# A hybrid GLA and SSD layer on one core: two projections moved ahead in the fill queue, mask building moved between two loops

## The chip, the cores and the metric

The kernel runs on one core of one Trainium2 chip. Its time is device microseconds from start to end of one launch; the median of three runs of the kernel before is 1287.27 us. One further execution was profiled, and all durations below are from it. The engines are TensorE (PE; PEld is its weight load), VectorE (DVE), ScalarE (ACT), GpSimd (POOL) and SyncE (SP, which issues the DMAs).

## What is computed

One layer over 1024 latent tokens (d_model 1024) with a prefix of 256 context tokens. Normed and modulated tokens go through one input projection; its columns feed a gated linear attention (GLA, 4 heads) and an SSD (Mamba-2, 8 heads in 2 groups), both in both directions, and an output projection and a SwiGLU follow. Cut to the parts that matter here:

```python
def hybrid_mixer(h_ctx, h_lat, rows, w_in, ...):
    # q, k, v, r, lr, z, xbc, dt_raw = split(h @ w_in)
    fc = _stream_features(h_ctx, ...)
    fl = _stream_features(h_lat, ...)
    gla_c, gla_l = _bidir(_gla_scan, ...)   # q, k, v, gates g from lr
    ssd_c, ssd_l = _bidir(_ssd_scan, ...)   # conv + silu of xbc, step sizes dt
    ...
    return y_ctx, _merge_heads(fl, gla_l, ssd_l, ...)   # gated by r and z, normed, @ w_out
```

The step sizes are `dt = softplus(dt_raw + bias)`, the SSD decays are made from `a = dt * -exp(a_log)` and its running sums, and the GLA gates are `log_sigmoid(lr @ wg + bg) / 16`.

## The kernel before, in words

Products keep float32 accuracy by splitting each operand in a high and a low float16 part; one product is then three (`mm3`, lines 219 to 223). A projection of a 128-channel weight over 512 tokens is 24 such matmuls, and a unit of 128 tokens by 256 channels is 24 matmuls of half that length.

The work around the change runs in this order. (1) Conv inputs of the SSD (x4, x5, x0, x1) are projected. (2) From the projected step sizes (p48, line 694) DVE makes a chain of some 25 steps on 128x160 elements (lines 715 to 737) that ends in `av`. (3) `decays()` (line 557) transposes `lrt` on PE (L561) and multiplies `av` with triangular masks (L566 to L568); `decay_factors()` (line 579) goes on from there (L582, L598). (4) `level_masks()` (line 135) builds the 28 masks of the GLA's levels: two iotas, a copy of four triangles to float16 (L142), seven DVE steps (`bl`, L146) and 28 GpSimd products (`lvm`, L149). (5) The 3x3 convs run as taps: on DVE (L506), and for x5 as a ScalarE product (L518) and a GpSimd sum (L520). (6) For SSD group 0, `ssd_states` (line 843) makes 9 chunk states (first product L852), then `ssd_chunks` (line 863) goes over 8 chunks: scores (L875, L876), exp on ScalarE (L880), weights (L885, L887, L888), state products (L899) and the products with xsl, the finish (L913 to L919); after the fourth and the last chunk a norm (L925), after the sixth chunk and behind the loop a merge (`merge_T`, L627 to L630) of half the tokens each. (7) The same for group 1. (8) The GLA for each of two head pairs: gates (L1113 is the first product), levels, states, outputs.

Projections that aren't needed at once are put in a fill queue (`Feeder`, line 249). `F.fill(us)` takes units from its head until their nominal cost (2.6 us for a token unit, 5.2 for 512 tokens of a channel unit) exceeds the sum asked for; `F.need(name)` empties it up to that name. The numbers asked for stand in `FILLS` (line 41). Before, the queue holds z0 (8 units), k0 (5.2, 5.2, 2.6), q0 (5.2, 5.2), z1 (8), later r0 and r1 (8 each), then v0 (10 units). The first fill is 4.6 us behind the third conv input, then 2 us for each of group 0's states and 3.2 us for each of its chunks, 1.0 and 2.5 for group 1's.

A fill unit's result goes to one of two PSUM banks ("pf", `psum_f`, line 78); ScalarE copies it out (L311 for token units, L320 for channel units). z's units are copied into tiles of the tag "zg", which has two buffers of four units each:

```python
zg[g].append(ssd.tile([P, 4, 256], F32, tag="zg", bufs=2, name=f"zg{g}"))
...
qk_units(0)
z_unit(1)
st0 = ssd_states(0, FILLS[0])
F.need("z0")
```

z0 is held there, gated and normed in place, until its half is merged. The order on each engine is fixed when the program is built: a scheduler goes over the program in order and may let an instruction pass others when its buffers and inputs would be ready. On the chip each engine's instructions run in that order. The other tags that matter are "dk" (two buffers, SSD skip term; the masks' iotas use it), "xw" (three, weighted inputs; the masks' `bl` uses it), "wst" (three staged weights) and "whl" (four split weights).

Of the kernel before, what the change touches and what calls it, by code (L numbers as in the profile page):

```python
# [16 lines left out]
P = 128  # L17
D = 1024
KT = D // P
T = 1024  # L20
# [17 lines left out]
SL = 2048.0  # L38
SG = 16.0
EG = 1.0 / (16 * SG)  # L40
FILLS = (2, 1.0, 3.2, 2.5, 4.6, 3.4, 8, 8.0, 0.5, 4.6, 4, 5.0, 2.7, 3.4, 4.0)


@with_exitstack
def dit_layer_kernel(
# [89 lines left out]
    def level_masks():  # L135
        xi = ssd.tile([P, P], I32, tag="dk", bufs=2, name="xi2")
        xj = ssd.tile([P, P], I32, tag="dk", bufs=2, name="xj2")
        G.iota(xi, [[1, P]], base=0, channel_multiplier=0)
        G.iota(xj, [[0, P]], base=0, channel_multiplier=1)
        V.tensor_tensor(xi, xi, xj, ALU.bitwise_xor)  # L140
        for i, nm in enumerate(("le", "ge", "gt", "lt")):
            G.tensor_copy(t16[:, i], tri[nm])  # L142
        for li in range(7):
            lv = 64 >> li
            bl = ssd.tile([P, P], F16, tag="xw", bufs=3, name="bl")
            V.tensor_scalar(bl, xi, float(lv), None, ALU.is_lt)  # L146
            b4 = bl.rearrange("p (n a l) -> p n a l", a=2, l=lv)
            for i, (d, x, a) in enumerate(((0, 0, 1), (1, 0, 0), (0, 1, 0), (1, 1, 1))):
                G.tensor_tensor(lvm[:, li, d, x].rearrange("p (n l) -> p n l", l=lv),  # L149
                                t16[:, i].rearrange("p (n a l) -> p n a l", a=2, l=lv)[:, :, a], b4[:, :, a], MUL)  # L150
# [93 lines left out]
    def load_ch(c0, name):  # L244
        return load_w(w_in[:, c0:c0 + P], KT, P, name)
# [11 lines left out]
    class Feeder:  # L257
# [13 lines left out]
        def step(self):  # L271
            if self.cur is None:
                self._preload()
                if not self.ready:
                    return None
                self.cur = self.ready.pop()
                self._preload()
            cost = next(self.cur[1], None)
            if cost is None:
                self.done.add(self.cur[0])  # L280
                self.cur = None
                return 0.0
            return cost

        def fill(self, us):
            self.owed += us
# [240 lines left out]
    def conv_ctx(m, w):  # L527
        xc = ssd.tile([P, TC], F32, tag="xc", bufs=2, name=f"xc{m}")
        ps = proj_ch(w, *CTX, psum_f())
        S.activation(xc, ps[:, :256], AF.Copy, scale=INV)  # L530
        xcs[m] = xc
# [25 lines left out]
    def decays():  # L557
        for t0, t1 in ((0, 8), (8, 10)):
            ps = psum((P, 1024), F16)
            for t in range(t0, t1):  # L560
                PE.transpose(ps[:96, (t - t0) * P:(t - t0 + 1) * P], lrt[:, t, :], ident16)  # L561
            S.copy(LRT[:, t0 * P:t1 * P], ps[:96, :(t1 - t0) * P])
        pcs = psum()
        pc = pcs[:, :480].rearrange("p (a d n h) -> p a d n h", a=3, d=2, h=8)
        for d, (i_nm, e_nm) in enumerate((("le", "gt"), ("ge", "lt"))):
            PE.matmul(pcs[:, 80 * d:80 * d + 80], tri[i_nm], av80[:, d], start=True, stop=True)  # L566
            PE.matmul(pcs[:, 160 + 80 * d:240 + 80 * d], tri[e_nm], av80[:, d], start=True, stop=True)
            PE.matmul(pcs[:, 320 + 80 * d:400 + 80 * d], ones, av80[:, d], start=True, stop=True)  # L568
        S.activation(ecum, pc[:, 0], AF.Exp)
        S.activation(wdec, pc[:, 1], AF.Exp)  # L570
        for g in range(2):
            hg = slice(4 * g, 4 * g + 4)
            S.activation(etg[0:64, g], pc[0:64, 2, 0, 0:9, hg], AF.Exp)
            S.activation(etg[64:128, g, 0:2], pc[64:128, 2, 1, 1::-1, hg], AF.Exp)
            S.activation(etg[64:128, g, 2:9], pc[64:128, 2, 1, 9:2:-1, hg], AF.Exp)
        V.tensor_tensor(wdec, wdec, dt, MUL)

    def decay_factors():

        pcc = psum()[:, :128].rearrange("p (d n g h) -> p d n g h", d=2, n=NL, g=2)  # L580
        for d in range(2):
            PE.matmul(pcc[:, d], tric[d], e1[:, d, NC_CTX:], start=True, stop=True)  # L582
        X = ssd.tile([P, NL, 2, 2, 2, 4], F32, tag="Eh", bufs=2, name="X")
        rX = ssd.tile([P, 64, 4], F32, tag="Eh", bufs=2, name="rX")
        A = ssd.tile([P, 64, 4, 4], F16, tag="ti", bufs=2, name="A")
        for d in range(2):
            V.tensor_copy(X[:, :, :, d, 0], pcc[:, d])
            V.tensor_tensor(X[:, :, :, d, 1], lnd[:, d].rearrange("p n (g h) -> p n g h", g=2), X[:, :, :, d, 0], SUB)
        x64 = X.rearrange("p n g d y h -> p (n g d y) h")
        V.memset(A[:, :, 3], 0.0)  # L590
        S.copy(A[:, :, 0], x64)
        V.tensor_tensor(rX, x64, A[:, :, 0], SUB)
        S.activation(A[:, :, 1], rX, AF.Copy, scale=SL)
        V.scalar_tensor_tensor(A[:, :, 2], rX, SL, A[:, :, 1], MUL, SUB)
        a2 = A.rearrange("p (n q) s h -> p n (q s h)", n=NL)
        pT = psum((P, T), F16)
        for n in range(NL):
            PE.transpose(pT[:, n * P:(n + 1) * P], a2[:, n], ident16)  # L598
        S.activation(Lw, pT, AF.Identity, scale=isG, bias=cF)
        for h in range(4):  # L600
            S.activation(Rr[:, :, h], pT.rearrange("p (n i) -> p n i", i=P), AF.Identity, scale=hF[h], bias=hG[h])
# [89 lines left out]
    for t in list(range(2, 10)) + [0, 1]:  # L691
        for k in range(KT):
            src, o = (hc[k], t * P) if t < NC_CTX else (hl[k], (t - NC_CTX) * P)
            mm3(p48[:, t, :], src[:, 0, o:o + P], src[:, 1, o:o + P], w48[:, 0, k, :], w48[:, 1, k, :],
                k == 0, k == KT - 1)

    conv_ctx(4, wx[4])
    conv_ctx(0, wx[0])
    dt = feat.tile([P, 2, NCH, 8], F32, name="dt")
# [46 lines left out]
    V.tensor_scalar(e1, av, -250.0, None, ALU.max)  # L746

    wx[2] = load_ch(O_X + 2 * P, "x2")
    decays()
    decay_factors()  # L750
    level_masks()
    acc0, tp = taps(0)
    acc5, tp5 = taps(5, True)
    for a, b in zip(tp[:4], tp5[:4]):
# [48 lines left out]
    def z_silu(g):  # L803
        for z in zg[g]:
            tc.keep_in_program_order(S.activation(z, z, AF.Silu))

    qT, kT = [None, None], [None, None]

    def qk_units(p):
        def kd():  # L810
            if kT[p] is None:
                kT[p] = feat.tile([P, TT], F32, tag="kT", bufs=1, name=f"kT{p}")
            return kT[p]

        def qd():
            if qT[p] is None:
                qT[p] = feat.tile([P, T], F32, tag="qT", bufs=1, name=f"qT{p}")
            return _shift(qT[p])
        ch_unit(kd, O_K + p * P, (LAT0, LAT1, CTX), INV, f"k{p}")
        ch_unit(qd, O_Q + p * P, (LAT0, LAT1), INV * 0.125, f"q{p}")  # L820

    class _shift:


        def __init__(self, t):
            self.t = t

        def __getitem__(self, i):
            return self.t[i[0], i[1].start - TC:i[1].stop - TC]

    z_unit(0)
    new_xs(0)
# [118 lines left out]
        norm(1)  # L951
        return lambda: merge(1)

    qk_units(0)
    z_unit(1)
    st0 = ssd_states(0, FILLS[0])
    F.need("z0")
# [10 lines left out]

    tc.keep_in_program_order(S.preload_act_table_set(LN_EXP))
    last = ssd_chunks(0, st0, FILLS[2], side0)  # L970
    F.fill(FILLS[5])
    last()
    while sidew:
# [906 lines left out]
```

## Time and profile before

| | us |
|---|---|
| median of 3 runs (1281.62 to 1289.43) | 1287.27 |
| the profiled execution | 1286.45 |
| its span, first to last instruction | 1284.7 |
| PE busy | 1189.7 (93%) |
| DVE busy | 897.4 (70%) |
| ACT busy | 602.4 (47%) |
| POOL busy | 249.5 (19%) |

Busy time overlaps between engines, and matmuls overlap each other, so a row is an engine's own time, not a share of the whole. A stretch in which one engine is busy all the time is bound by it; where none is, the waits say which one is late. PEclk in the rows below is the granted clock of TensorE as a share of 2.4 GHz; 0.50 is 1.2 GHz.

### The profile page before, as it was taken

The numbers are of one execution on the slowest core, as the hardware profiler recorded it, in microseconds if no ns is written. First come the engines' busy times: TensorE is split into PE (matmuls) and PEld (weight loads), VectorE is DVE, ScalarE is ACT, GpSimd is POOL, SyncE is SP. The second block draws the span as 40 slices with busy tenths as digits, with TensorE's granted clock in tenths as the row PEclk, the third lists the DMA queues.
The fourth block names the chain that finished last, engine by engine and source line by source line (L and its number), as shares of the span: only waits on it lengthen the run. The fifth ranks groups of instructions, "written<-read, shape, count | busy, mean of one in ns | idle before, by whom it ended". The sixth has DMA issues, their size and how long they took to land. (4 is left out here: it accounts for less than half of the span.)

```text
span 1284.7 us, 21607 instructions
## 1 busy us (share of the span) xinstructions
PE 1189.7 (93%) x8684; PEld 673.5 (52%) x8684; DVE 897.4 (70%) x1486; ACT 602.4 (47%) x1158; POOL 249.5 (19%) x233
## 2 busy tenths in 40 slices
PE   5994899999999998999986899999999999999997
PEld 3553575767876697644442344444444444444444
DVE  8589796758378356776799865787775557754447
ACT  5345725545585464444673343444543334343433
POOL 0228032142000000001265211212211111300011
PEclk9997799999999999998988999999999999999999
DMA  9710211011201003488314522555532226320425
GB/s 307 215 29 17 70 30 50 18 34 46 95 6 35 1 3 100 149 285 303 117 50 148 179 91 74 164 184 176 181 115 67 66 81 212 133 91 17 148 75 203
DMA packets 90753, 140.20 MB, mean 109 GB/s; under 512 B 7592, under 2 KB 61597, under 8 KB 90653
## 3 DMA queue, kind: packets, MB, share of 16 engines
q1 hardware_dynamic: 90653, 138.82, 33.0%
q8 instruction: 68, 1.11, 0.4%
q14 instruction: 32, 0.26, 0.1%
HBM read 117.31 MB, written 20.97 MB: 108 GB/s over the span
## 5 line engine op out<-in xcount | busy, mean ns | idle before, releaser
L221 PE MATMUL ps<-T,wS 128*128 128x512 f16 x264 | 101.9, 386 | 10.5 <-DVE u L1612 7.0
L222 PE MATMUL ps<-T,wS 128*128 128x512 f16 x264 | 102.0, 386 | 4.0 <-DVE T L1441 4.0
L223 PE MATMUL ps<-T,wS 128*128 128x512 f16 x264 | 101.8, 386 | 0.0
L1722 DVE TENSOR_TENSOR ah<-hid,ah 128x512 f16<-128x512 f32 x66 | 50.6, 769 | 54.4 <-ACT ah L1721 54.4
L1501 DVE SCALAR_TENSOR_TENSOR wS<-S,wS 128x512 f16<-128x512 f32 x88 | 67.2, 777 | 27.9 <-ACT wS L1500 27.8
L1500 ACT ACTIVATE wS<-S 128x512 f16<-128x512 f32 x88 | 54.4, 628 | 56.9 <-PE ps L223 30.4
L1721 ACT CAST ah<-hid 128x512 f16<-128x512 f32 x66 | 40.5, 618 | 85.3 <-PE ps L223 46.5
L1501 DVE SCALAR_TENSOR_TENSOR wA<-wst,wA 128x512 f16<-128x512 f32 x66 | 55.9, 849 | 25.5 <-ACT wA L1500 25.4
L1500 ACT ACTIVATE wA<-wst 128x512 f16<-128x512 f32 x66 | 41.3, 628 | 54.4 <-PE ps L223 35.2
L222 PEld LDWEIGHTS <-wS 128*128 128x128 f16 x352 | 34.9, 99 | 55.1 <-issue 15.9
L221 PEld LDWEIGHTS <-wS 128*128 128x128 f16 x352 | 34.9, 99 | 50.7 <-DVE u L1612 7.6
L223 PEld LDWEIGHTS <-wS 128*128 128x128 f16 x352 | 34.9, 99 | 47.6 <-issue 7.5
L1517 POOL TENSOR_TENSOR S<-wst,S 128x512 f32<-128x512 f32 x22 | 32.6, 1483 | 137.2 <-DVE S L1516 91.5
L1515 POOL TENSOR_TENSOR S<-wst 128x512 f32<-128x512 f32 x22 | 31.0, 1409 | 117.3 <-DVE wS L1501 100.3
L506 DVE SCALAR_TENSOR_TENSOR acc<-xin,cwcol,acc 128x945 f32<-128x945 f32 (+2 forms) x40 | 48.9, 1240 | 0.4
L221 PEld LDWEIGHTS <-hl 128*128 128x128 f16 x448 | 42.5, 97 | 8.3 <-issue 3.1
L222 PEld LDWEIGHTS <-hl 128*128 128x128 f16 x448 | 42.5, 97 | 4.8 <-issue 0.8
L223 PEld LDWEIGHTS <-hl 128*128 128x128 f16 x448 | 42.5, 97 | 4.7 <-issue 0.4
L222 PEld LDWEIGHTS <-wA 128*128 128x128 f16 x264 | 25.9, 98 | 35.6 <-issue 5.2
L221 PE MATMUL ps<-wo,oT 128*128 128x512 f16 x112 | 44.2, 395 | 0.0
L222 PE MATMUL ps<-wo,oT 128*128 128x512 f16 x112 | 44.0, 393 | 0.0
L223 PE MATMUL ps<-wo,oT 128*128 128x512 f16 x112 | 43.8, 391 | 0.0
(540 smaller groups left out, 3539.0 us busy)
## 6 DMA issues: line engine op xcount, KB each, us to landing
wmst<-in_w_mod_dram SPq DMA_DIRECT2D x32, 512.0 KB, 4.8
wst<-in_w_gate_dram SPq DMA_DIRECT2D x26, 512.0 KB, 4.3
wst<-in_w_up_dram SPq DMA_DIRECT2D x26, 512.0 KB, 3.7
wdb<-in_w_down_dram SPq DMA_DIRECT2D x22, 512.0 KB, 5.6
x<-in_x_dram SPq DMA_DIRECT2D x16, 512.0 KB, 6.6
wm<-in_w_mod_dram SPq DMA_DIRECT2D x8, 1024.0 KB, 10.4
t32d<-wdt SPq DMA_DIRECT2D x11, 512.0 KB, 3.0
t14d<-wdt SPq DMA_DIRECT2D x11, 512.0 KB, 4.5
```

The costliest lines, as they stand in the source:

```text
L221: PE.matmul(ps, lh, rh, start=start, stop=False, skip_group_check=on)
L222: PE.matmul(ps, lh, rl, start=False, stop=False, skip_group_check=on)
L223: PE.matmul(ps, ll, rh, start=False, stop=stop, skip_group_check=on)
L506: V.scalar_tensor_tensor(acr[:, r0:r1, q0:q1], xr[:, r0 + dr:r1 + dr, q0 + dc:q1 + dc], cw, acr[:, r0:r1, q0:q1], MUL, ADD)
L1500: S.activation(w[:, 0], src, AF.Copy, scale=SW)
L1501: V.scalar_tensor_tensor(w[:, 1], src, SW, w[:, 0], MUL, SUB)
L1515: G.tensor_tensor(s3, b["A11"], b["A21"], SUB)
L1517: G.tensor_tensor(s4, b["A12"], s2, SUB)
L1721: S.copy(dst[:, 0], src)
L1722: V.tensor_tensor(dst[:, 1], src, dst[:, 0], SUB)
```

## The change

k0 and q0 lead the fill queue (their loads are begun at once, `step_ahead`), 13 us of fill are asked for ahead of `decays()` and 5 us behind it, the four triangle copies are taken out of `level_masks()`, and `level_masks()` is called behind group 0's loop, before its last merge.

```diff
-FILLS = (2, 1.0, 3.2, 2.5, 4.6, 3.4, 8, 8.0, 0.5, 4.6, 4, 5.0, 2.7, 3.4, 4.0)
+FILLS = (2, 1.0, 3.2, 2.5, 4.6, 3.4, 8, 8.0, 0.5, 4.6, 4, 5.0, 2.7, 3.4, 4.0, 5.0, 13.0)
...
         V.tensor_tensor(xi, xi, xj, ALU.bitwise_xor)
-        for i, nm in enumerate(("le", "ge", "gt", "lt")):
-            G.tensor_copy(t16[:, i], tri[nm])
         for li in range(7):
...
+        def step_ahead(self):
+
+            self._preload()
...
+    qT, kT = [None, None], [None, None]
+
+    def qk_units(p):
...
+    qk_units(0)
+    F.step_ahead()
     conv_ctx(4, wx[4])
     conv_ctx(0, wx[0])
...
     wx[2] = load_ch(O_X + 2 * P, "x2")
+    F.fill(FILLS[16])
     decays()
+    for i, nm in enumerate(("le", "ge", "gt", "lt")):
+        G.tensor_copy(t16[:, i], tri[nm])
+    F.fill(FILLS[15])
     decay_factors()
-    level_masks()
     acc0, tp = taps(0)
...
-    qk_units(0)
     z_unit(1)
     st0 = ssd_states(0, FILLS[0])
...
     last = ssd_chunks(0, st0, FILLS[2], side0)
+    level_masks()
     F.fill(FILLS[5])
     last()
```

`qk_units` and `_shift` are moved up in the text as they are. The lines of the kernel after differ by a few: L566 is L568 there, L627 is L629, L899 is L906, L1092 is L1099.

On PE around the decay products, the kernel before: `w_x_1300` is the weight of conv input x2, `av` the end of DVE's chain.

```order
L223 MATMUL pf<-hl_169,w_x_1300 128x512
L566 MATMUL ps<-av,trs 128x80
L567 MATMUL ps<-av,trs 128x80
L568 MATMUL ps<-av,ones 128x80
...
L582 MATMUL ps<-sp_1255,trs 128x64 x2
L221 LDWEIGHTS w_x_1300
L221 MATMUL pf<-hl_162,w_x_1300 128x512
```

The same place in the kernel after: `w_k_1193` and `w_q_1310` are the weights of k0 and q0, `w_x_796` that of x1, whose context part stood ahead of the decay products before.

```order
L221 MATMUL pf<-hc_171,w_k_1193 128x256
L563 LDWEIGHTS lrt
L563 MATMUL ps<-ident_81,lrt 96x128
...
L568 MATMUL ps<-av,trs 128x80
L569 MATMUL ps<-av,trs 128x80
L570 MATMUL ps<-av,ones 128x80
...
L219 LDWEIGHTS w_q_1310
L219 MATMUL pf<-hl_162,w_q_1310 128x512
...
L584 MATMUL ps<-sp_1260,trs 128x64 x2
L219 LDWEIGHTS w_x_796
L219 MATMUL pf<-hc_170,w_x_796 128x256
```

All of k0 (72 matmuls) now stands ahead of the decay products and the first half of q0 (24) behind them; the context part of x1 (24) and the first half of x2 (24) moved from ahead of them to behind.

On PE at the seventh and eighth chunk of group 0, the kernel after (`zg_1885` is the first half of z0, `w_z_0_1852` and `w_z_4_1857` are the two parts of z1's weight):

```order
L629 MATMUL ps<-ident,zg_1885 128x128 x4
L883 MATMUL ps<-cmc,bmc 128x128
L906 MATMUL ps<-st_1831,cmc 128x256
L906 MATMUL ps<-st_1831,cmd 128x256
L219 LDWEIGHTS hl_162
L219 MATMUL pf<-w_z_0_1852,hl_162 128x256
...
L221 LDWEIGHTS hl_169
L221 MATMUL pf<-w_z_4_1857,hl_169 128x256
L219 LDWEIGHTS Eh
L219 MATMUL ps<-xsl_1830,Eh 128x64
```

In the kernel before the same place has one unit of z1 between the first merge and the state products:

```order
L627 MATMUL ps<-ident,zg_1754 128x128 x8
L875 LDWEIGHTS Lw
L875 MATMUL ps<-Rr,Lw 128x512
...
L876 MATMUL ps<-cmc,bmc 128x128
L221 LDWEIGHTS hl_162
L221 MATMUL pf<-w_z_0_2250,hl_162 128x256
```

Between the state products (L906) and the products with xsl stand 96 matmuls of z1, four units, where the kernel before has none; between the scores of the third and of the eighth chunk, where it has one piece of k0, both of q0 and a unit of z1, there is no fill now.

On DVE at the end of group 1, the kernel before (`rv_y`, `ry_y` are the norm, `w_k_5183` and `w_q_5188` the weights of pair 1, `wg` the gate weights):

```order
L201 SCALAR_TENSOR_TENSOR ry_y_3638<-rt_y_3639,ry_y_3638 128x4
L630 SCALAR_TENSOR_TENSOR oT_3498<-ps,ncol,oT_3498 128x512
L630 SCALAR_TENSOR_TENSOR oT_3506<-ps,ncol,oT_3506 128x512
L216 SCALAR_TENSOR_TENSOR w_k_5183<-st_k_5181,w_k_5183 128x1024
L216 SCALAR_TENSOR_TENSOR w_q_5188<-st_q_5186,w_q_5188 128x1024
L1092 MEMSET wg_3785 96x512
L1097 TENSOR_SCALAR W_3793<-wg_3785 96x512
```

And the kernel after:

```order
L214 SCALAR_TENSOR_TENSOR w_k_5183<-st_k_5181,w_k_5183 128x1024
L920 TENSOR_TENSOR ti<-ps,ecum 128x256 x2
L214 SCALAR_TENSOR_TENSOR w_q_5188<-st_q_5186,w_q_5188 128x1024
...
L199 SCALAR_TENSOR_TENSOR ry_y_3750<-rt_y_3751,ry_y_3750 128x4
L1099 MEMSET wg_3785 96x512
L632 SCALAR_TENSOR_TENSOR oT_3610<-ps,ncol,oT_3610 128x512
L632 SCALAR_TENSOR_TENSOR oT_3618<-ps,ncol,oT_3618 128x512
L311 TENSOR_SCALAR v_3799<-pf 128x256
L1104 TENSOR_SCALAR W_3793<-wg_3785 96x512
```

The two splits moved into the last chunk, and the memset ahead of the merge's last steps.

## Rows read from the trace of the kernel before

**Rows 1.** Busy (instructions) by stretch: PE, PEld, DVE, ACT, POOL; PEclk, DMA share, GB/s.
```profile
92.00:112.00 20.00, 16.34 (x151) 11.82 (x147) 17.80 (x32) 12.18 (x17) 19.31 (x38) 0.91 0.10 27
112.00:127.40 15.40, 0.63 (x3) 0.12 (x2) 15.13 (x21) 6.43 (x7) 12.87 (x10) 0.64 0.00 0
127.40:146.00 18.60, 14.40 (x83) 10.07 (x84) 13.13 (x24) 16.71 (x30) 1.88 (x1) 0.78 0.00 1
146.00:174.00 28.00, 28.00 (x157) 18.66 (x155) 23.60 (x27) 12.42 (x21) 0.43 (x1) 0.80 0.43 113
...
203.30:246.60 43.30, 42.45 (x339) 25.32 (x339) 34.16 (x69) 24.41 (x49) 8.76 (x13) 1.00 0.08 25
...
264.00:323.70 59.70, 56.58 (x486) 39.00 (x487) 46.49 (x94) 28.25 (x62) 22.43 (x28) 1.00 0.14 39
323.70:348.50 24.80, 23.48 (x216) 20.76 (x213) 8.33 (x17) 13.75 (x25) 0.72 (x1) 1.00 0.22 64
```

**Rows 2.** Waits from 92 to 172 us; us in total, times, longest.
```profile
PE ps L566 <- DVE av L737: 14.8, 1, 14.8
...
PE pf L221 <- ACT w_x L215: 4.2, 1, 4.2
```

**Rows 3.** Busy time for tiles w_k (two rows), w_q, w_z, w_r; engines PE, PEld, DVE, ACT, or PE, DVE, ACT.
```profile
92.00:174.00 82.00, 0.00 (x0) 0.00 (x0) 1.23 (x1) 1.07 (x1) 0.79 0.17 45
174.00:264.00 90.00, 13.50 (x72) 6.81 (x72) 0.00 (x0) 0.00 (x0) 1.00 0.10 27
...
174.00:264.00 90.00, 10.71 (x48) 4.53 (x48) 0.00 (x0) 0.00 (x0) 1.00 0.10 27
...
92.00:174.00 82.00, 5.67 (x49) 2.44 (x2) 2.06 (x2) 0.79 0.17 45
...
323.70:349.00 25.30, 10.70 (x96) 0.00 (x0) 0.00 (x0) 1.00 0.22 66
```

**Rows 4.** Groups of 95 to 128 us (DVE), 92 to 174 (POOL); then DVE's timeline.
```profile
L146 DVE TENSOR_SCALAR bl<-xi 128x128 f16<-128x128 int32 x7 | 6.0, 851 | 0.5 <-POOL lvm L149 0.5
...
L149 POOL TENSOR_TENSOR lvm<-t,bl 128x64 f16<-128x64 f16 x28 | 12.5, 479 | 0.0
...
99.33 2.24 DVE L146 TENSOR_SCALAR bl<-xi 128x128 f16<-128x128 int32 x1
...
102.28 0.33 DVE L146 TENSOR_SCALAR bl<-xi 128x128 f16<-128x128 int32 x1
...
110.19 0.45 DVE L732 TENSOR_TENSOR sp<-sp,sp 128x160 f32<-128x160 f32 x1
...
125.60 0.32 DVE L732 TENSOR_TENSOR sp<-sp,sp 128x160 f32<-128x160 f32 x1
```

**Rows 5.** Timeline of PE, and of DVE for L888; start us, us, instruction.
```profile
100.00 0.27 PE L223 MATMUL pf<-hc,w_x 128*128 128x256 f16 x1
102.41 1.03 PE L561 MATMUL ps<-ident,lrt 128*96 128x128 f16 x10 [2.14 <-DVE lrt L724]
...
220.74 0.69 DVE L888 TENSOR_TENSOR Eh<-E,Eh 128x512 f16<-128x512 f32 x1 [0.68 <-ACT Eh L887]
...
229.13 0.68 DVE L888 TENSOR_TENSOR Eh<-E,Eh 128x512 f16<-128x512 f32 x1
...
251.72 0.49 PE L627 MATMUL ps<-ident,zg 128*128 128x128 f32 x3
```

**Rows 6.** Busy time by stretch behind the wait for `av`.
```profile
128.00:132.00 4.00, 4.00 (x18) 3.30 (x18) 0.91 (x6) 2.87 (x11) 0.00 (x0) 0.50 0.00 0
132.00:136.00 4.00, 4.00 (x16) 1.66 (x15) 2.50 (x4) 3.97 (x6) 1.88 (x1) 0.82 0.00 0
```

**Rows 7.** DVE's timeline at the end of group 1; in brackets the idle time before.
```profile
339.34 1.23 DVE L216 SCALAR_TENSOR_TENSOR w_k<-st_k,w_k 128x1024 f16<-128x1024 f32 x1 [5.12 <-ACT w_k L215]
...
347.24 0.42 DVE L1097 TENSOR_SCALAR W<-wg 96x512 f16<-96x512 f32 x1 [5.00 <-DMA wg<-in_gla_wg_b_dram]
...
350.60 1.29 DVE L1117 SCALAR_TENSOR_TENSOR gx<-ps,bt 128x512 f32<-128x512 f32 x2 [2.22 <-DMA bt<-in_gla_bg_b_dram]
```

More of the change, by code (lines that the diff above doesn't have):

```diff
@@ L695, in dit_layer_kernel, with kd, qd, __init__ @@
                 k == 0, k == KT - 1)
+    qT, kT = [None, None], [None, None]
+    def qk_units(p):
+        def kd():
+            if kT[p] is None:
+                kT[p] = feat.tile([P, TT], F32, tag="kT", bufs=1, name=f"kT{p}")
+            return kT[p]
+        def qd():
+            if qT[p] is None:
+                qT[p] = feat.tile([P, T], F32, tag="qT", bufs=1, name=f"qT{p}")
+            return _shift(qT[p])
+        ch_unit(kd, O_K + p * P, (LAT0, LAT1, CTX), INV, f"k{p}")
+        ch_unit(qd, O_Q + p * P, (LAT0, LAT1), INV * 0.125, f"q{p}")
+    class _shift:
+        def __init__(self, t):
+            self.t = t
+        def __getitem__(self, i):
+            return self.t[i[0], i[1].start - TC:i[1].stop - TC]
+    qk_units(0)
+    F.step_ahead()
     conv_ctx(4, wx[4])
@@ L805, in z_silu @@
             tc.keep_in_program_order(S.activation(z, z, AF.Silu))
[L807 to L829, printed above, removed]
     z_unit(0)
```

## The prediction

> **What bounds the kernel now.** I read the times by stage first, then the waits of the stretch that the change touches, then single engines inside it. By stage [rows 1], TensorE (PE) is nearly always busy from 146 us on and idle in one place: 0.63 us of work in the 15.4 us from 112 to 127.4, and 14.40 of 18.6 us behind it. The granted clock is 0.64, 0.78 and 0.80 in the stretches from 112 to 174 and 1.00 in those behind, so part of the work there runs at 1.2 GHz. The waits [rows 2] name the cause: 14.8 us in which the first decay product (L566) waits for `av`, the end of VectorE's (DVE's) chain of small steps, with all of PE's queue behind it; and 4.2 us for the split of the next conv weight. DVE is full there, 15.13 of 15.4 us [rows 1]. So 92 to 174 is bound by DVE and by PE's order; from 174 to 324 PE is the bound, as each gap of the SSD loops is filled with projections.
>
> **The change part by part.** It takes the projections of k and q of the first pair out of the loop of SSD group 0 and puts them before and behind the decay products: 13.50 and 10.71 us of PE [rows 3], 24.2 together. The masks leave the same stretch. The total work stays; only idle time and slow clock can be won. The sum goes along PE's order, by the profiled execution (1286.45 us: a span of 1284.7 and 1.75 around it; the median of the three runs is 0.8 above it).
>
> *First, the end of DVE's chain (127.4 us).* Seven mask steps, 6.0 us, go [rows 4]; the splits of k's and q's weights come in, 1.23 us each [rows 3]; net -3.5. Small DVE steps beside GpSimd's mask products are a little longer: L732 takes 0.45 us at 110 and 0.32 at 125.6 [rows 4]; some eight such steps are under the masks, so -1. I take `av` at 123.0, 4.4 us earlier. It can't help PE below 114.8, since k keeps PE until then (context products end at 100.3, k 13.5, the transposes L561 1.0 [rows 3, 5]); from the other side, GpSimd's eight conv steps stay, under which a DVE step is stretched (2.24 us against 0.33 for the same step [rows 4]), and they may bunch so that nothing is gained: 127.4.
> On this the Trainium skill (SBUF — State Buffer, Who interferes with whom) says that a DVE step with two SBUF inputs and a GpSimd step that reads SBUF take one shared port in turn, each for its whole length. [...] By the rule each of the 28 mask products (0.48 us) would also stop a DVE step beside it, for half its length on average, 0.24 us and not the measured 0.13; `av` would come some 1 us earlier still and the forecast would be 1 us lower. I go by the rows.
>
> *Second, from `av` to the first state product (174.0, where the fourth stretch of [rows 1] ends), 46.6 us before.* PE gets both halves of q there (10.7), and of what it did ahead of `av` before, the context conv of x1 (as k's context part, 13.50 - 10.71 = 2.8) and half of a projection like q's (5.4); two units of z0 go, 5.7 us [rows 3]: together +13.2. The wait of 4.2 us goes, since the conv weight is split far ahead in the new order. The slow clock goes in part: 0.78 over 18.6 us and 0.80 over 28 us [rows 1] are 8.2 and 11.2 us at the lower level; 15.2 of them are not the wait itself and cost half, 7.6 us. PE still idles some 8 us ahead of `av`, so the slow start repeats (0.50 and 0.82 in the two stretches behind the wait [rows 6]); I leave 2.7 of it: -4.9. Sum +4.1, so the first state product stands at 174.0 - 4.4 + 4.1 = 173.7. **Term: -0.3 us**, with k and q done.
> k's and q's loads go ahead of z's on SP's queue; the DMA share is 0.10 and 0.00 where they land [rows 1], so that costs nothing.
>
> *Third, the states of group 0* have 141 products of z in place of 143, and 48 before the first scores in place of k's 24 double-length ones. Nothing changes.
>
> *Fourth, the loop of group 0 and its end (203.3 to 264 us).* Here the fill is missing, and not replaced. z1's results go to the two zg buffers that z0 holds until each half is merged, so with two pf banks only two units can be done before the first merge. The order shows it: two units at the head of the loop, four between the seventh chunk's state products and its last products, two behind the second merge. With nothing between, a chunk goes at the pace of DVE and the waits between engines. DVE has 34.16 us in the loop [rows 1], by my count 5.0 of them for splits, merge and norm: 3.7 per chunk. From the fourth to the sixth L888, the one place where two chunks' products stand on PE without fill between, there are 8.4 us [rows 5], 4.2 per chunk. I take 4.2; the bounds are 3.7 and the 5.4 of now (43.3 / 8). The first products come 7.2 us after the first scores, the seventh's at 7.2 + 5.5 x 4.2 = 30.3; four units of 24 products, 2.8 us each, and the last two outputs: 42.5. From there to the second merge 5.1 us as now (246.6 to 251.72 [rows 5]), and 0.9 for the masks' first steps, which stand among the norm's on DVE: 48.5. It came at 48.4. Behind it PE has two units of z and four of r, 144 products of 0.111 us (r's 96 take 10.70 [rows 3]), 16.0, and 4.4 for merge, transposes and the first xw: group 1 starts at 68.9 against 60.7. **Term: +8.2 us.** In return 98 products of r are done, against 8.
> The masks, 12.5 us on GpSimd [rows 4], are done at about 62, ahead of group 1's xw, so they cost nothing; without that cover xw would wait for what is left of them.
>
> *Fifth, group 1* (59.7 us [rows 1]): the same fills, 8 products more: **+0.9 us**.
>
> *Sixth, from the last outputs of group 1 to the first gate product L1113 (323.7 to 348.5, 24.8 us [rows 1]).* Before, 96 products of r and 109 of v stand here; now 80 of v, 8.9 us, with the merge 10.0. What is late next is the gate weight. Its memset on DVE stood behind the splits of k1 and q1, which waited 5.12 us for ScalarE [rows 7]; in the new order these are done in the loop and the memset follows the norm: 4.4 us for the norm, 0.5, 5.0 for the loads (the wait of L1097 [rows 7]), 1.2 for W, with the issues 12.0. **Term: 12.0 - 24.8 = -12.8 us.**
>
> *Seventh, the gates.* The bias load goes ahead of the weights on SP's queue, so of the wait of 2.22 us at L1117 [rows 7] 1.5 go; 29 products of v (3.2 us) are left over and run among the levels, where some gaps take 1.0 of them: **+0.7 us**. Behind this everything is as before and shifts.
>
> Sum: -0.3 + 8.2 + 0.9 - 12.8 + 0.7 = -3.3, that is 1283 us. Of the 30 us that were idle (22.6 by [rows 1]) or slow (7.6) ahead of 174, most come back as idle time in the loop, where PE has some 2 us of work in a chunk of 4.2.
>
> **The rivals.**
> A. *The fill moves over whole*: the loop runs at DVE's 3.7 us, and the last outputs don't wait for the four z units. For it: DVE is busy for only 79% of the loop. Against it: PE's order is fixed and has these units ahead of the outputs. It takes off up to 11.2 us: 1272.
> B. *The z1 units jam PE, and it is slower than before*: units three to six need pf banks that ScalarE empties only when the first half is merged. If that merge comes 1.5 chunks later than I think, the four units, and both last outputs behind them in PE's queue, come 1.5 x 4.2 = 6.3 us later: +3.0, 1289.5. It decides if the second merge comes later than 52 us behind the first scores. For it: ScalarE's order has the two evacuations behind the norm's four scalings; against it: they stand ahead of the merge's own copies.
> C. *DVE's chain is not shorter*, as GpSimd's conv steps stretch other steps instead: `av` at 127.4, +4.4: 1287.5, no change.
>
> **How the numbers follow.** Forecast 0.45 (its own range 1278 to 1289), A 0.18, B 0.17, C 0.20. By the bounds of the chunk's pace alone (5.5 chunks of 3.7 to 5.4 us) the time is 1280 to 1290. The range, 1271 to 1294, leaves out the far half of A and the tail of B. A measurement of this kernel tells about 1% (12.9 us) from no change: faster 0.14 (most of A), slower 0.04 (B with group 1 late as well), within 1% 0.82.
>
> **What would show it.** Right: PE's wait ahead of the decay products falls from 14.8 to about 8 us and `av` ends near 123; the first state product stays within 2 us of 174; PE's busy share in group 0's loop falls from 98% to some 75%; group 1 starts 7 to 9 us later than before; L1113 comes 3 to 4 us earlier. Wrong: group 1 starts no later than before (A), the second merge comes over 52 us behind the first scores (B), or `av` ends at 127 (C).

## The result and the profile after

The changed kernel takes 1296.08 us in the median (1294.41 to 1297.61); beside it the kernel before takes 1287.48. The ratio is 1.0069 with a 95% interval of 1.0054 to 1.0084: slower, by 0.7%. The forecast was 1283 us, a little faster, with 1294 as the end of its range. The profiled execution took 1294.93 us, with a span of 1293.2 against 1284.7.

One point serves as a yardstick below: the first product of `kht` (gated keys times v, where the states of the GLA begin; L1188 before, L1195 after). Up to there PE has done the same work in either kernel: z, r, v, k and q of the first pair and both SSD groups. By stage, the kernel before (columns as in [rows 1]; the stretches are group 0 from its first scores to group 1's first state product, group 1's last outputs, that is the last products with xsl, to the first `kht` product, and the whole way from 92 us):

```profile
203.30:264.10 60.80, 59.61 (x494) 40.69 (x493) 40.92 (x82) 34.74 (x74) 9.94 (x15) 1.00 0.08 23
323.75:386.80 63.05, 58.53 (x957) 51.13 (x954) 35.40 (x54) 43.77 (x84) 0.72 (x1) 1.00 0.16 52
92.00:386.80 294.80, 262.32 (x2527) 189.76 (x2522) 216.74 (x362) 162.82 (x304) 83.70 (x106) 0.94 0.14 40
```

The kernel after, with the stretch up to the first state product ahead:

```profile
92.00:173.50 81.50, 68.83 (x445) 43.09 (x446) 66.19 (x90) 50.38 (x75) 23.16 (x19) 0.94 0.19 52
203.00:274.80 71.80, 64.83 (x488) 47.27 (x487) 41.05 (x90) 32.80 (x73) 19.64 (x45) 0.81 0.11 30
334.60:393.50 58.90, 51.73 (x863) 43.80 (x860) 37.21 (x59) 41.78 (x81) 0.72 (x1) 0.91 0.16 46
92.00:393.50 301.50, 270.70 (x2507) 193.94 (x2507) 213.78 (x361) 161.50 (x301) 79.04 (x106) 0.92 0.14 39
```

The whole way grew from 294.8 to 301.5 us, by 6.7. PE's idle time in it did not grow (294.8 - 262.3 = 32.5 before, 30.8 after); PE was busy for 8.4 us more with nearly the same products (the cut at 92 us falls at another one). The extra busy time is half clock: the granted clock over the way fell from 0.94 to 0.92, and it moved. Whether that is also the cause of the loss is tested below. Ahead of the first state product it rose (0.79 over 82 us [rows 3], 0.94 after); in group 0's stretch it fell from 1.00 to 0.81, and behind group 1 from 1.00 to 0.91. The first of these two stretches is 11.0 us longer than before. The other is only 4.2 us shorter, although 96 products of r, 10.7 us, have left it.

The start went as forecast. Of PE's waits from 92 to 172 us, the two that answer to [rows 2]:

```profile
PE ps L568 <- DVE av L765: 9.7, 1, 9.7
PE pf L219 <- ACT xc L532: 1.7, 1, 1.7
```

The wait for `av` fell from 14.8 to 9.7 us, the wait of 4.2 us for the conv weight is gone. Group 0's loop from its first scores on, in short stretches:

```profile
203.00:210.00 7.00, 7.00 (x59) 5.38 (x58) 4.73 (x7) 6.09 (x8) 0.00 (x0) 1.00 0.26 77
210.00:216.00 6.00, 4.90 (x46) 2.82 (x46) 6.00 (x14) 2.38 (x6) 2.18 (x3) 1.00 0.28 87
216.00:222.00 6.00, 5.57 (x35) 3.00 (x34) 6.00 (x14) 2.29 (x5) 2.43 (x3) 0.56 0.00 0
222.00:228.00 6.00, 6.00 (x28) 3.23 (x26) 6.00 (x15) 3.26 (x9) 2.87 (x4) 0.50 0.00 0
228.00:234.50 6.50, 6.30 (x31) 3.10 (x30) 4.51 (x14) 4.65 (x12) 1.46 (x2) 0.50 0.01 3
234.50:240.00 5.50, 5.50 (x40) 4.45 (x40) 3.49 (x7) 2.26 (x6) 1.39 (x2) 0.76 0.00 0
240.00:248.00 8.00, 7.86 (x87) 6.69 (x85) 1.20 (x4) 0.38 (x1) 0.00 (x0) 1.00 0.01 2
248.00:253.00 5.00, 0.10 (x1) 0.11 (x1) 3.63 (x14) 2.19 (x8) 2.26 (x7) 0.78 0.00 0
253.00:258.00 5.00, 5.00 (x24) 3.70 (x25) 2.58 (x6) 3.11 (x8) 5.00 (x20) 0.54 0.00 0
```

This table is the heart of the case. Up to 210 us PE still has two units of z1. From 210 to 228 DVE is busy without a gap (18.0 of 18.0 us) and PE has nothing but the chunks' own small products; the granted clock goes to 0.56 and then 0.50, so PE looks busy (11.57 of 12 us from 216 to 228) with work that would fill half of that. From 234.5 to 248 it is the other way round: PE works through four units of z1 and DVE is busy for 4.7 of 13.5 us. From 248 to 253 PE waits for the second merge's norm, and from 253 on it is mostly PE again, with the work that the queue could not run earlier. That z1 waits for room is seen on ScalarE, which copies the first two units out of their banks at 233 us, behind the first merge's transposes (L629), though PE ended them at 206.5 and 210.0:

```profile
233.07 0.66 ACT L313 ACTIVATE zg<-pf 128x256 f32<-128x256 f32 x2 [1.47 <-PE ps L629]
```

Before, both kinds of work stood side by side (42.45 of 43.30 us of PE beside 34.16 of DVE [rows 1]); now they stand one after the other.

PE's timeline at three points (start, duration, then the wait in brackets), the second merge of group 0, the first gate product and the first `kht` product:

```profile
252.90 2.15 PE L629 MATMUL ps<-ident,zg 128*128 128x128 f32 x8 [5.04 <-ACT zg L932]
...
353.97 1.04 PE L1120 MATMUL ps<-W,LRT 96*128 96x256 f16 x8
...
393.46 0.77 PE L1195 MATMUL ps<-v,kht 128*64 128x128 f32 x10
```

And DVE's timeline at the end of group 1, where [rows 7] had the memset behind the splits:

```profile
334.64 0.42 DVE L925 TENSOR_TENSOR zg<-zg,ti 128x256 f32<-128x256 f32 x1
334.98 1.22 DVE L214 SCALAR_TENSOR_TENSOR w_k<-st_k,w_k 128x1024 f16<-128x1024 f32 x1
...
336.93 1.55 DVE L214 SCALAR_TENSOR_TENSOR w_q<-st_q,w_q 128x1024 f16<-128x1024 f32 x1
...
342.43 0.16 DVE L199 SCALAR_TENSOR_TENSOR ry_y<-rt_y,ry_y 128x4 f32<-128x4 f32 x1
345.80 0.48 DVE L1099 MEMSET wg<- 96x512 f32 x1 [3.22 <-PE ps L629]
...
351.65 0.42 DVE L1104 TENSOR_SCALAR W<-wg 96x512 f16<-96x512 f32 x1 [3.79 <-DMA wg<-in_gla_wg_b_dram]
```

The splits of k1 and q1 (L214) stand inside the last chunk, ahead of the norm's last step (L199, 342.43), and the memset of the gate weight waits 3.22 us for L629, the transposes of the merge. From the gate product to `kht` PE has next to no gap any more:

```profile
353.97:393.46 39.49, 38.20 (x774) 33.16 (x771) 27.74 (x39) 30.16 (x60) 0.00 (x0) 1.00 0.02 5
```

### The profile page after: what moved, and what is told of

It reads as the page before. It is cut to its first block, busy times and chain, and to the rows that moved or that the text cites. A ratio compares the mean times of both kernels' runs of the same rounds, so it can differ in the third digit from the quotient of the medians.

```text
span 1293.2 us, 21601 instructions
## 1 busy us (share of the span) xinstructions
PE 1198.6 (93%) x8684; PEld 676.4 (52%) x8684; DVE 896.7 (69%) x1487; ACT 601.3 (46%) x1157; POOL 246.3 (19%) x233
## 5 line engine op out<-in xcount | busy, mean ns | idle before, releaser
L220 PE MATMUL ps<-wo,oT 128*128 128x512 f16 x112 | 45.1, 402 | 0.0
L219 PE MATMUL ps<-wo,oT 128*128 128x512 f16 x112 | 45.0, 402 | 0.0
L221 PE MATMUL ps<-wo,oT 128*128 128x512 f16 x112 | 44.7, 399 | 0.0
```

The lines of the kernel that those rows point to most:

```text
L219: PE.matmul(ps, lh, rh, start=start, stop=False, skip_group_check=on)
L220: PE.matmul(ps, lh, rl, start=False, stop=False, skip_group_check=on)
L221: PE.matmul(ps, ll, rh, start=False, stop=stop, skip_group_check=on)
```

## The experiments

They ran in three series, each on one chip and each beside the kernel before, whose median was 1290.1, 1290.9 and 1290.9 us there; ratios are to it. The kernel before, profiled once more, was up to 1.5 us earlier ahead of the first state product (`av` ended at 126.0 against 127.4), kept the times of the trace shown within 0.8 us from there to 640 us, and was 3.5 us later at the end of the MLP's weight steps (last L1501 at 1057.3 against 1053.8). So times from the first state product to 640 us are compared directly, `av` to no better than 1.5 us, and whole times by ratio.

**The two kernels again.**

> The kernel before, unchanged, for a profile beside the others. All theories: up to 640 us within 1 us of the trace shown (first gate product near 348.5); if the chip is the cause of the 5 us that the four profiles so far lose between 640 and 1055, this one loses them too.

> The changed kernel, unchanged, for a profile on the chip of these runs. All theories: first kh product (L1195) within 1 us of 393.5, loop at +71 to +72.5, span 1296 to 1298, as the kernel before was 3.4 us longer here.

Measured: the kernel before, span 1288.1, first gate product 348.6, first `kht` product 386.3; the changed kernel, span 1296.9, `kht` 394.1, group 0's stretch 71.6 us. Both as expected; the loss is 7.8 us at `kht` and 8.8 at the end, so nearly all of it arises up to there.

**The masks alone.** The kernel before with

```diff
-        for i, nm in enumerate(("le", "ge", "gt", "lt")):
-            G.tensor_copy(t16[:, i], tri[nm])
...
     decays()
+    for i, nm in enumerate(("le", "ge", "gt", "lt")):
+        G.tensor_copy(t16[:, i], tri[nm])
     decay_factors()
-    level_masks()
...
     last = ssd_chunks(0, st0, FILLS[2], side0)
+    level_masks()
```

> The kernel before with only the masks (and the four casts) moved behind group 0's loop; k and q stay in the loop. Theory (the loss is the fill taken out of the loop, the masks are harmless): av ends 3 to 4 us earlier, near 124; the first state product some 3 us earlier than 174.0; group 0's loop and the end of group 1 keep their lengths (60.7 and 24.8 us); time 1283 to 1285. Rival (the masks' steps behind the loop cost: DVE's mask steps among the norm, GpSimd's products ahead of group 1's products): the stretch from the first scores to group 1's first state product is 3 us or more longer than 60.7, and the time is 1287 or more.

Measured: ratio 0.9989 (0.9977 to 1.0001). `av` ended at 121.2, the first state product came at 168.3, 5.7 us earlier; group 0's stretch took 61.4 us, the one from group 1's last outputs to the first gate product 25.1.

```profile
92.00:168.30 76.30, 58.20 (x370) 40.09 (x370) 64.97 (x88) 47.34 (x71) 22.17 (x18) 0.82 0.19 49
197.60:259.00 61.40, 60.01 (x494) 40.76 (x493) 42.79 (x90) 34.80 (x74) 18.01 (x45) 1.00 0.08 23
92.00:381.60 289.60, 261.55 (x2505) 189.19 (x2505) 213.96 (x359) 162.43 (x302) 79.36 (x105) 0.95 0.14 41
```

The rival falls: behind the loop the masks cost 0.6 us. What they win ahead of it is more than expected, 5.7 us, and 5.2 of it are there at the first `kht` product (381.6 for 386.8). At the end the ratio leaves 1.4 us (0.0011 of 1290), with an interval from nothing to 3.0, so the 2 to 4 us that were forecast are not confirmed. Beside the second profile of the kernel before, the lead is 4.7 us at `kht`, 5.0 at 550 us, 2.7 at 570 and 1.9 from 930 on: most of what is lost goes between the second head pair's last merge and the MLP's first weight step. What takes it there is not shown.

**The lead alone.** The changed kernel with `level_masks()` back behind `decay_factors()`.

> The changed kernel with the masks back in their old place, k and q still leading. Theory (the masks' move wins 4 us at av and costs nothing): av near 127.5, PE's wait ahead of the decay products some 14 us in place of 9.7, the first state product near 177, loop and end as in the changed kernel; time 1298 to 1301. Rival (the masks behind the loop cost what is lost): group 1 starts under 9 us later than in the kernel before, and the time is 1293 or less.

Measured: ratio 1.0104 (1.0084 to 1.0123), 1303.1 us. `av` 127.9, first state product 178.2, `kht` 397.0, group 0's stretch 70.8. As the theory had it, with a first state product 1 us later still; only PE's wait ahead of the decay products was not the 14 us expected but 9.2, with another 3.2 inside k's projection. So the loss belongs to the lead of k and q, and the masks take some 4 us off it (ratios 1.0104 and 1.0069).

**The gate weight early.** The changed kernel with a staging buffer for weight and bias, loaded ahead of group 1's loop:

```diff
+    stg = wp.tile([P, 1024], F32, tag="wst", bufs=3, name="stg")
+    wg32 = stg[:96, 0:512].rearrange("p (d n) -> p d n", d=2)
+    V.memset(wg32, 0.0)
...
     F.need("z1")
     z_silu(1)
...
+    G.tensor_copy(bt, bts)
```

> The changed kernel with the gate weight and the bias loaded into a staging buffer ahead of group 1's loop, so that only the split of W and a copy of the bias stand behind the merge. Theory (W's chain of memset behind the merge, loads of 5 us and split sets the first gate product): it comes at 346 to 349 in place of 354.0, and the time is 1288 to 1291. Rival (the products of v at the lower clock, behind the wait for a pf bank, set it): the first gate product stays at 352 or later, time 1294 to 1297.

Measured: ratio 1.0084 (1.0059 to 1.0110). The first gate product (L1123 here) came at 350.8, 3.2 us earlier than in the changed kernel, and the first `kht` product (L1198) at 395.6, no earlier (393.5 and 394.1 in the two profiles of the changed kernel). This run stood 1 us later already at group 0's first scores; counted from group 1's last outputs the gate product came at 15.2 us for 19.3, and `kht` at 59.9 for 58.8. PE's timeline:

```profile
350.84 1.04 PE L1123 MATMUL ps<-W,LRT 96*128 96x256 f16 x8
...
355.69 0.27 PE L219 MATMUL pf<-w_v,hl 128*128 128x256 f16 x1 [2.93 <-ACT v L313]
...
395.58 1.09 PE L1198 MATMUL ps<-v,kht 128*64 128x128 f32 x16
```

Both numbers of the theory fail, and the rival's as well. W's chain was a real wait, but behind the gates PE now stands 2.93 us for ScalarE, which empties v's bank among the gates' own steps, and 2.3 us more for the gates, where the changed kernel has no such wait; and all of v must still be done ahead of `kht`. The gate product was the wrong place to count a gain at.

**Fill put back into the loop.** r's second half goes out to DRAM by a small buffer and needs no room that the loop holds:

```diff
+    r1_unit()
     z_unit(1)
     st0 = ssd_states(0, FILLS[0])
...
     r_unit(0)
-    r1_unit()
```

> The changed kernel with r's second half (whose results go out to DRAM by a small buffer) put ahead of z1 in the fill queue, so that group 0's loop has a unit of fill in each chunk again. Theory (the loop without fill is the loss): PE is busy for 95% or more of the loop at a granted clock of 1.00, group 1's first state product comes at 263 to 266 in place of 274.8, the end of group 1 takes some 19 us as in the changed kernel; time 1284 to 1287. Rival (the work is only shifted, the idle time turns up in another place before the gates): the first gate product stays at 352 or later, time 1293 to 1297.

Measured: ratio 0.9960 (0.9947 to 0.9973), some 14 us less than the changed kernel's 1.0069.

```profile
203.50:268.10 64.60, 62.88 (x589) 49.82 (x588) 44.46 (x92) 35.73 (x79) 17.94 (x45) 1.00 0.19 55
268.10:380.30 112.20, 99.38 (x1250) 73.73 (x1250) 78.96 (x146) 67.12 (x133) 23.66 (x29) 0.94 0.11 30
```

PE is busy for 97% of group 0's stretch at a clock of 1.00. Its first state product of group 1 came at 268.1, two us later than expected, but with four units of r more done by then (589 products for 488), and the way behind it is 112.2 us in place of 118.7; the first gate product came at 341.0, 15.4 us behind group 1's last outputs and not the 19 expected. The lead is unchanged here; only the order of the queue behind it is another. So the lead as such does not cost; what costs is the queue that stands still in the loop.

**The half clock.** The changed kernel with products that nobody reads, 12 a chunk of group 0 and 40 ahead of its second merge:

```diff
+            if g == 0:
+                for _ in range(12):
+                    PE.matmul(py[:, 256:512], hl[0][:, 0, 0:P], hl[1][:, 0, 0:256], start=True, stop=True,
+                              skip_group_check=True)
...
+    warm(40)
     level_masks()
```

> The changed kernel with products whose results nobody reads, 12 a chunk in group 0's loop and 40 ahead of its second merge, so that TensorE doesn't stand idle there. Theory (part of the loss is the half clock that the idle loop brings): granted clock 1.00 from the first scores to group 1, group 1's first state product at +67 to +69 behind the first scores in place of +71.8; ratio to the kernel before 1.003 to 1.005. Rival (the loop waits for VectorE and for buffers, its clock costs nothing): +71 to +74, ratio 1.007 or more.

Measured: ratio 1.0052 (1.0035 to 1.0068), group 0's stretch 71.4 us.

```profile
203.50:274.90 71.40, 69.92 (x624) 56.04 (x623) 41.40 (x90) 32.46 (x73) 18.61 (x45) 0.98 0.11 31
```

By the loop the rival is right, by the ratio the truth lies between the two. The clock was 0.98, the 136 products took some 15 us (0.111 us each), and the stretch was 0.4 us shorter, not longer. So about 15 us of PE's time in it is waiting, which the half clock had covered up. The price of the clock itself isn't settled by this: the four units of z1 took 10.7 us here for 11.9, but the products also stood in the way of the chunks' outputs, the last of which ended at 250.3 against 247.9.

The same at the end of group 1, on the run with r1 in the loop (28 products ahead of the second merge, 18 among and behind its transposes):

> r1 in group 0's loop as in the run before, and 46 products that nobody reads about the second merge of group 1, where TensorE stood idle for some 7 us and worked at half clock for 13. Theory (the half clock there costs 3 us): the first gate product at 336 to 339 in place of 341.0, ratio 0.992 to 0.995. Rival (ScalarE and VectorE, which empty v's banks and make the gates, set the pace there): what is won at the gate is lost before the first kh products, ratio 0.995 to 0.998.

Measured: ratio 0.9942 (0.9924 to 0.9961), first gate product 339.1, `kht` 378.6 against 380.3.

```profile
268.30:378.60 110.30, 100.86 (x1295) 76.18 (x1295) 79.03 (x146) 66.84 (x133) 23.69 (x29) 1.00 0.10 31
```

There the half clock (0.94 over the whole stretch in the run before, 1.00 here) is worth 1.7 to 1.9 us, a little less than expected; the ratios' intervals overlap.

**The dose of the lead.** Only k's first 512 columns lead, the rest of k and q stays in the loop:

```diff
+        if p == 0 and part == 0:
+            ch_unit(kd, O_K + p * P, (LAT0,), INV, "k0a")
+            return
...
-    F.fill(FILLS[16])
+    F.fill(5.0)
     decays()
...
-    F.fill(FILLS[15])
     decay_factors()
...
+    qk_units(0)
     z_unit(1)
```

> A smaller dose: masks moved, but only k's first 512 columns lead (5.35 us, which fit into the wait for av); the rest of k and q stay in group 0's loop. Theory (the lead pays as long as the loop keeps enough fill): the loop loses 5 us of work without idle time, group 1's first state product at +55 to +58 behind the first scores in place of +60.8, the first gate product at 337 to 340, ratio 0.993 to 0.996. Rival (each unit taken out of the loop comes back as idle time): +60 to +62, ratio 0.998 or more.

Measured: ratio 0.9929 (0.9913 to 0.9944), 1281.55 us. First state product 165.7 (168.3 with the masks alone), group 0's stretch 62.5 us, first gate product 335.1, `kht` 375.8.

```profile
92.00:165.70 73.70, 58.25 (x397) 39.19 (x398) 60.94 (x85) 48.11 (x72) 23.58 (x20) 0.88 0.22 58
195.10:257.60 62.50, 59.65 (x511) 42.16 (x510) 42.23 (x90) 34.13 (x74) 18.86 (x45) 1.00 0.16 42
92.00:375.80 283.80, 256.12 (x2507) 185.06 (x2507) 216.19 (x362) 161.94 (x302) 81.54 (x106) 0.97 0.16 43
```

Better than expected at the gates, for another reason: the loop did not get shorter (there the rival's figure was the nearer one). But it did not fall idle either: it stayed full (95% at 1.00), and the place of the missing unit was taken by z and r. The next dose, both blocks of k (`(LAT0, LAT1)` and a fill of 10 us):

> A dose between the half lead and the change: both 512 columns of k lead (10.7 us), k's context part and q stay in the loop. Theory (a lead pays up to the wait for av, of which the half lead left 8.1 us, and costs where the loop's chunks go without fill): first state product at 164 to 166, wait ahead of the decay products under 4 us, group 1's first state product at +64 to +67 behind the first scores, first kh product at 376 to 380 in place of the half lead's 375.8; ratio 0.993 to 0.997. Rival (the wait alone counts): +60 to +63, kh at 370 to 373, ratio 0.988 to 0.991.

Measured: ratio 1.0066 (1.0042 to 1.0091), group 0's stretch 73.1, `kht` 393.5. The expectation is missed on all counts, on the bad side. PE's wait ahead of the decay products, first with one block, then with two:

```profile
PE ps L568 <- DVE av L768: 8.1, 1, 8.1
```

```profile
PE ps L568 <- DVE av L768: 11.4, 1, 11.4
```

The second block did not go into the wait. In PE's order it stands in the place of 26 products of x1's and x2's conv weights that stood there with one block, and these go behind `av`; the first state product is 6.1 us later. And with one unit less in the loop, z1's first two units come two chunks earlier, ahead of the third and fourth outputs. There the queue stands still until the first merge frees z's buffers. All of k (13.5 us, q in the loop):

> All of k leads (13.5 us), q stays in the loop. Theory as for the dose below it: +66 to +69, kh at 379 to 385, ratio 0.996 to 1.001. Rival (the wait alone counts): kh at 370 to 374, ratio 0.988 to 0.992.

Measured: ratio 1.0038 (1.0022 to 1.0055), group 0's stretch 72.2, `kht` 391.9; worse than expected, and again close to the changed kernel. So the cost isn't in proportion to the dose: two chunks without fill (two blocks of k) bring as much of it as three (all of k) or five (the changed kernel). What the three bad kernels have in common is z1 at the head of the queue too early. The test of that is the run with two blocks of k, and four tiles of r's second half ahead of z1:

```diff
+    r1_unit(range(2, 6), "r1a")
     z_unit(1)
```

> As the run with both 512 columns of k, and the first four tiles of r's second half put ahead of z1 in the queue, so that the loop has a unit in each chunk. Theory (it is the empty chunks that cost): PE busy for 95% or more of the loop at a granted clock of 1.00, +60 to +63 with more of r done, kh at 370 to 375, ratio 0.987 to 0.992. Rival (the loop's length is set by VectorE and the norm, whatever PE does meanwhile): kh as in the run without r1a, ratio within 0.002 of it.

Measured: ratio 0.9925 (0.9902 to 0.9948), `kht` 379.5. Up to 225 us the two kernels are in step (group 0's first scores at 199.6 and 199.1). From there, first without r1a, then with it:

```profile
225.00:235.00 10.00, 8.51 (x48) 4.46 (x48) 8.36 (x23) 5.34 (x14) 2.89 (x4) 0.77 0.01 2
235.00:247.00 12.00, 12.00 (x101) 10.14 (x100) 3.79 (x8) 3.84 (x11) 1.23 (x2) 0.91 0.00 0
247.00:272.70 25.70, 20.39 (x182) 17.09 (x178) 10.77 (x28) 11.04 (x27) 9.98 (x33) 0.87 0.17 42
92.00:393.50 301.50, 268.51 (x2507) 193.20 (x2507) 218.14 (x363) 161.82 (x302) 77.52 (x106) 0.92 0.15 41
```

```profile
225.00:235.00 10.00, 10.00 (x103) 7.83 (x100) 8.06 (x19) 7.06 (x18) 2.29 (x4) 1.00 0.05 19
235.00:247.00 12.00, 11.22 (x113) 8.56 (x110) 10.37 (x22) 4.80 (x12) 2.98 (x5) 1.00 0.33 97
247.00:261.20 14.20, 12.60 (x113) 10.87 (x111) 5.10 (x18) 7.59 (x20) 8.34 (x30) 1.00 0.01 2
92.00:379.50 287.50, 261.60 (x2505) 188.97 (x2505) 219.49 (x364) 164.03 (x304) 77.35 (x106) 0.95 0.17 46
```

From 225 to 235 us PE has 48 products beside DVE's steps in the one, 103 in the other. From 235 to 247 it works through four units of z1 in a lump in the one, and DVE, whose outputs stand behind them, is busy for 3.79 of 12 us; in the other DVE is busy for 10.37. PE's wait for the norm ahead of the second merge is 5.1 us in the one (5.0 in the changed kernel) and 1.4 in the other (1.7 with one block of k). Group 0's stretch shrinks from 73.1 to 62.1 us with the same 511 products, the whole way by 14.0. The `kht` product is later than the expected 370 to 375, since the first state product is as late as without r1a. This run, the one with one block of k and the two with all of r's second half in the loop are faster than both kernels. Two things stay open. In every bad run the chunks without fill and the lump of z1 behind them come together, so no run tells what each costs alone; and no run gave z1 a third buffer, which would test the reason for the standstill directly.

## Why the prediction was wrong

| step of the prediction | forecast | measured |
|---|---|---|
| decay products begin (`av`) | 123.0 | 123.3 |
| PE's wait ahead of them | about 8 | 9.7 |
| first state product | 173.7, term -0.3 | 173.5, -0.5 |
| group 0, first scores to group 1 | 68.9, term +8.2 | 71.8, +11.0 |
| group 1 | term +0.9 | +0.1 |
| last outputs to the gate product | 12.0, term -12.8 | 19.4, -5.4 |
| gates and behind | +0.7 | +3.0 |

*First and second step: right*, in `av`, in the wait and in the first state product. On the shared port, the forecast went by the rows (123.0) and named 122 as what the Trainium skill's rule (SBUF — State Buffer, Who interferes with whom) would make of it; the first decay product at 123.3, and 123.9 to 124.4 in the runs with the same lead, lie nearer to the rows, but 1 us is less than the 1.5 by which `av` differed between two profiles of the kernel before, so the runs do not decide it. The stretched step of 2.24 us in [rows 4] (`bl<-xi`) has one input, so it says nothing of a rule for steps with two. In the kernel before, GpSimd's later conv steps stretch both kinds alike, one input (L733, 0.24 us without them) and two (L732, 0.32):

```profile
120.43 2.23 DVE L733 TENSOR_SCALAR sp<-sp 128x160 f32<-128x160 f32 x1
122.97 2.32 DVE L732 TENSOR_TENSOR sp<-sp,sp 128x160 f32<-128x160 f32 x1
```

*Fourth step: the mechanism right, the size off by 2.8 us.* The pace of a chunk was taken as 4.2 us; DVE, full from 210 to 228, set 3.6 (last products of the first chunk at 210.5, of the sixth at 228.5). That alone would have brought the last outputs 3 us earlier than forecast; they ended 2.4 us later (44.9 us behind the first scores for 42.5). All was reckoned at full clock. From 228 to 234.5, ahead of the four units of z1, the first merge's transposes and the seventh chunk's scores ran at 0.50; the four units took 11.9 us for 11.2 (clock 0.76 up to 240 us); and behind the last outputs the second merge's transposes took 2.15 us for the 1.04 that eight of them take at full clock, and the two units behind them 6.3 for 5.4. That a full clock would have won it back is not shown (71.4 us with the products that nobody reads). The sign named for this step, PE's busy share at 75%, did not come either, since the half clock made short work long: 93% from 210 to 234.5.

*Sixth step: this one failed.* The term said that with r out of the way the end of group 1 would take the 12.0 us that the gate weight needs, "-12.8"; the gate product, forecast 3 to 4 us earlier, came 5.5 later. The 7.4 us between 12.0 and 19.4 are these. The splits of k1 and q1, "done in the loop" by the prediction, stood in the last chunk (1.22 and 1.55 us) and with them the norm ended 8.0 us behind the last outputs, not 4.4: 3.6. The memset did not follow the norm but waited for the merge's transposes: 3.2. Behind the loads W was ready at 352.8, and the gate product stood 1.2 us more behind products of v; these are the remaining 0.6, with the loads a little longer. In these waits PE fell to half clock (0.50 from 344 to 351), so the 32 products of v ahead of the gate product took 6.2 us. And the run with the early gate weight shows that the term was wrong in kind: it got 3 to 4 us of this back at the gate and won nothing at `kht`. Counted to `kht`, the sum of the sixth and seventh term would have been -12.1; it was -4.2: r's products took 10.7 us with them, but PE's remaining work took 3.9 us longer at a clock of 0.91 over the stretch (51.7 us for 58.5 - 10.7), and its idle time grew by 2.7 (7.2 for 4.5).

*Seventh step*: the part up to `kht` held (+1.2 us); 29 products of v more than before stand between the gate product and `kht` (160 for 131), as forecast. Some 2 us of the end's loss arise behind `kht`, between 550 and 620 us, and were not forecast; their cause stays open.

*The rivals.* A had DVE's pace right and its sum wrong. B named what the loop suffers from, units of z1 that stand ahead of the outputs, but its sign did not come (second merge 49.9 us behind the first scores, under 52). C fell. None had the half clock in the loop. The jam that B speaks of is the one that the order of z1 and r decides; B let it cost 6.3 us and only if a merge came late, in the runs it costs 11 in group 0's stretch and 14 up to `kht` with the merge in time.

The whole in one sentence: the lead and the masks' move won 5 us of PE's wait ahead of the decay products, but for that the lead took from group 0's loop the work that PE did beside DVE's, and r, which could have filled it, stood in the queue behind z1, whose buffers come free only at the first merge. The Trainium skill (Perfetto Trace Analysis, Identifying Performance Opportunities) says both things in general: where the most-contended engine changes over time, interleaving the stretches can help, and a gap that repeats can mean that the next tile finds no room. The pair of runs with and without r1a agrees with the first, 14.0 us by order alone; for the second there is z1's copy at 233 us, behind the merge, but no run with more room.

## What to carry to other kernels

Work that fills an engine's waits is worth most where another engine is the bound for long: before it is moved to fill one gap, go through the stretch that it leaves and ask of each chunk what can run there next, in the queue's order and with the buffers that are free then; one unit that finds no buffer holds up all behind it. Count a gain at the last point that all the moved work must pass (here `kht`), not at the first instruction that comes earlier. And look in the built order whether a lead goes into the gap at all: the second block of k went into the place of work that stood ahead of the gap already, and the wait grew from 8.1 to 11.4 us.

## What was new of the hardware

PE's clock fell to 0.50 while PE was counted busy for nearly all of the time, with small products and short gaps between them: 11.57 of 12 us from 216 to 228, behind 4.90 of 6 us from 210 to 216 at a clock of 1.00. With 12 further products a chunk the same stretch (216 to 234) ran at 0.91 and no chunk came earlier. So a busy share must be read beside the clock; here about half of it was slow work in time that was waiting anyway.

The kernel before took 3.4 us more in its second profile (spans of 1288.1 and 1284.7), and its median was 3 us higher in all three later series. Every one of the twelve later profiles, the changed kernel's second one too, loses 3 to 5.5 us between 800 and 960 us against the kernel before's first one, where weights stream in from DRAM; the changed kernel's first profile does not (8.0 us behind at 800, 8.4 at 960). So the difference goes with the series and not with the kernel; whether the chip makes it was not tried. A difference of 0.3% is therefore only read beside runs of the same series.
